# Two heads at a time in the attention and state space parts, and the last layer norm in a written order of VectorE

## The chip, the cores and the metric

One core of one Trainium2 chip runs the whole program in one launch. The metric is the device time in microseconds (us). The kernel before took 1444.42 us, the median of three runs (1443.53 to 1445.5).

## The reference

256 tokens of width 1024 pass through two blocks, all in f32.

The first block has two layers. Each takes a modulation vector from a condition (`w_ada`), normalizes, and runs a mixer whose one input projection feeds three parts; their outputs are concatenated, multiplied by `w_out`, and followed by an MLP with a squared relu.

```python
# differential attention: 4 heads, two softmaxes each over 32-wide q and k, values 64 wide
p = softmax(mask(q1 @ k1.T * scale)) - lam * softmax(mask(q2 @ k2.T * scale));  y_a = rmsnorm(p @ v)
# latent attention (MLA): 4 heads, scores of a 64-wide and a 32-wide rotary part
sc = (qn @ kn.T + qr @ kr.T) * scale;                  y_b = softmax(mask(sc)) @ v
# state space: 8 heads of 64, two groups, after a convolution, with a decay per head
y_c = ((cc @ bc.T) * exp(decay of the head)) @ (xs * dt) + ...
y = concatenate([y_a, y_b, y_c]) @ w_out
```

The mask lets a query see keys of its own and earlier chunks of 64. The second block runs three branches (an RWKV7 scan; attention of 8 heads of 64 with a distance penalty, called `moba`; a diagonal state space model), merges them with gates, and adds a layer norm, 32 experts in 4 groups with two chosen per token, and a last layer norm over the 1024 columns:

```python
y = (x - mean) * rsqrt(var + 1e-5) * w + b
```

## The kernel before

Tokens stand as columns (256 of them, `T`) and features as the 128 partitions (`P`) in most tensors; scores and the last layer norm have tokens on the partitions. Weights come from HBM on SP's queue in units of 1 MB (`raw`); ScalarE rounds each to a high part (`whi`) and VectorE subtracts to get the low part (`wlo`), and a product is three matmuls of these parts (`xh,whi`, `xh,wlo`, `xl,whi`). A *strip* is 128 output features, 24 such matmuls. Products without such parts are plain f32 matmuls, and each of those leaves two records on TensorE in the trace, one per pass; a bf16 matmul (the masks) leaves one.

The instructions of each engine are put in order by a planner, by what their operands wait for and by the place where they were traced. An instruction that is *pinned* (`pin`, L371) stays behind the instruction traced before it on its engine; `inorder(1)` pins TensorE's matmuls and transposes, `inorder()` pins all. All pass through helpers, whose lines are the ones that the profile shows: `act` L379 (ScalarE), `tt` L382, `ts` L386/387, `stt` L390 (VectorE), `mm` L393, `tr` L401 (TensorE).

A causal score matrix of 256 x 256 is kept as a tile of 128 x 384: 128 columns for the first half of the queries, 256 for the second. One head's scores are two f32 matmuls (`scores`, L925), 128 and 256 columns; the masks are two bf16 matmuls of one row (`chunkmask`, L919). `soft` (L910) takes two maxima on VectorE and two exponentials with accumulated sums on ScalarE. `pv` (L930) transposes the probabilities in three blocks, copies them out of PSUM by ScalarE (`at_pT`), and multiplies by the head's 64 value columns in two matmuls, into one half of the rows of an output tile `o`.

In the mixer (`_mixer`), the order of tracing is: input strips, the MLA projections, the state space matrix, the convolution with its transposes (`xd`), then MLA (L1130 to 1152), where after each two heads a strip of differential q and one of k are traced; a modulation vector (`adas`), the values v (`va`), the differential attention (L1175 to 1196), four strips of z, another modulation vector, and the state space heads (L1225 to 1246) with an exponent product `cs`, two masks, three exponentials, one multiplication (`ssE`) and two products each; then `w_out`. PSUM has eight buffers there, two each of the tags d (strips), s (scores), t (transposes) and o (outputs). `moba` (L1644) does the same for its heads, with a strip of q and of k before each two heads; after the scores there are two bf16 matmuls for the penalty (`mb_ak`) and two for the mask (`c4b`).

The tail of `moe` (L2612 to 2633) has the last layer norm, four quarters of 128 x 512 in PSUM (two halves of the tokens, `i`, by two halves of the columns, `h`). Statistics come first; for three quarters ScalarE subtracts the mean and GpSimd multiplies by w; then the reciprocal root (`rsqrt`, L556, a row of small VectorE steps in three rounds), and four fused operations add b, each with a write to HBM behind it, in the order (1,1), (0,0), (1,0), (0,1).

Of the kernel before, what the change touches and what calls it, by code (L numbers as in the profile page):

```python
# [26 lines left out]
BF = mybir.dt.bfloat16  # L27
I32 = mybir.dt.int32
AF = mybir.ActivationFunctionType
OP = mybir.AluOpType  # L30
# [4 lines left out]
P = 128  # L35
T = 256
# [275 lines left out]
class Prog:  # L312
# [603 lines left out]
        self.act(e[:, 0:P], sc[:, 0:P], AF.Exp, bias=mx[:, 0:1], scale=scale, accum=sm[:, j:j + 1])  # L916
        self.act(e[:, P:384], sc[:, P:384], AF.Exp, bias=mx[:, 1:2], scale=scale, accum=sm[:, j + 1:j + 2])

    def chunkmask(self, sc, r):  # L919

        for o in (0, 256):
            self.mm(sc[:, o:o + P], self.B("cm_q")[r:r + 1], self.B("cm_k")[r:r + 1], start=False, stop=True,
                    skip_group_check=True)

    def scores(self, sc, q, k, first, last=False):  # L925

        self.mm(sc[:, 0:P], q[:, 0:P], k[:, 0:P], start=first, stop=last, skip_group_check=True)
        self.mm(sc[:, P:384], q[:, P:T], k[:, 0:T], start=False, stop=last, skip_group_check=True)

    def pv(self, pool, p, v, vcol, o, half):  # L930

        tp = self.pt([P, 384], "t")
        for b in range(3):
            self.tr(tp[:, b * P:(b + 1) * P], p[:, b * P:(b + 1) * P])
        pT = self.sb(pool, [P, 384], "at_pT", bufs=2)

        self.act(pT, tp)
        oo = o[64 * half:64 * half + 64]
        self.mm(oo[:, 0:T], v[:, 0, vcol:vcol + 64], pT[:, 0:T], start=True, stop=False)
        self.mm(oo[:, P:T], v[:, 1, vcol:vcol + 64], pT[:, T:384], start=False, stop=True)  # L940


    def mixconst(self, l):
# [28 lines left out]
    def _mixer(self, pool, l, xT, pre, fill, n):  # L972
# [154 lines left out]
        sc96 = 96.0 ** -0.5  # L1127
        o = None

        def mla_head(h, o):  # L1130
            s, a = divmod(h, 2)
            sc = self.pt([P, 384], "s")
            r0 = slice(64 * a, 64 * a + 64)
            r1 = slice(32 * h, 32 * h + 32)
            self.scores(sc, qn[r0, s], kn[r0, s], True)
            self.scores(sc, qr[r1], krr[r1], False)
            self.chunkmask(sc, 32 * h)
# [6 lines left out]
            self.pv(pool, e, vb, 64 * h, o, a)  # L1144
# [29 lines left out]
        nsq = sb([P, 4, T], "nsq")  # L1174
        for s in range(2):  # L1175
            o = self.pt([P, T], "o")
            for a in range(2):
                sm = sb([P, 4], "at_s", bufs=3)
                es = []
                for m in range(2):  # L1180
                    sc = self.pt([P, 384], "s")
                    r = slice(64 * a + 32 * m, 64 * a + 32 * m + 32)
                    self.scores(sc, qa[r, s], ka[r, s], True)
                    self.chunkmask(sc, 64 * a + 32 * m)
                    e = sb([P, 384], "at_e", bufs=3)
                    self.soft(pool, sc, sc32, e, sm, 2 * m)
# [6 lines left out]
                self.pv(pool, es[0], va, 64 * (2 * s + a), o, a)  # L1193
# [30 lines left out]
        nsq = sb([P, 4, T], "nsq")  # L1224
        for s in range(4):  # L1225
            po = self.pt([P, T], "o")
            for a in range(2):
                h = 2 * s + a
                pe = self.pt([P, 384], "s")
                neg, idb = self.B("causnegT"), self.B("ident")  # L1230
                self.mm(pe, self.i8[0:40, h:h + 1].to_broadcast([40, P]), cs, start=True, stop=False,
                        skip_group_check=True)
                self.mm(pe[:, 0:P], idb, neg, start=False, stop=True, skip_group_check=True)
                self.mm(pe[:, T:384], idb, neg, start=False, stop=True, skip_group_check=True)
                E = sb([P, 384], "ssE", bufs=2)
                self.act(E[:, 0:P], pe[:, 0:P], AF.Exp, bias=nA[:, h:h + 1])
                self.act(E[:, P:T], pe[:, P:T], AF.Exp, bias=nA[:, 16 + h:17 + h])
                self.act(E[:, T:384], pe[:, T:384], AF.Exp, bias=nA[:, 8 + h:9 + h])
                self.tt(E, E, G[:, h // 4], OP.mult)
                oo = po[64 * a:64 * a + 64]  # L1240
                self.mm(oo, xd[:, 0, h], E[:, 0:T], start=True, stop=False, skip_group_check=True)
                self.mm(oo[:, P:T], xd[:, 1, h], E[:, T:384], start=False, stop=True,
                        skip_group_check=True)
            self.stt(yc[:, s], xbc[:, 2 + s], self.col(f"dskip{l}", s), po, OP.mult, OP.add)
            self.stt(yc[:, s], yc[:, s], 0.5, zs[:, s], OP.mult, OP.mult)
            self.act(nsq[:, s], yc[:, s], AF.Square)
# [397 lines left out]
    def moba(self, pool, X, y):  # L1644
# [6 lines left out]
        for s in range(4):  # L1651
# [4 lines left out]
            ps = self.strip(("in2", 2304 + P * s), X)  # L1656
            nc.vector.tensor_copy(k, ps)
            o = self.pt([P, T], "o")
            for a in range(2):
                h = 2 * s + a  # L1660
                r = slice(64 * a, 64 * a + 64)
                sc = self.pt([P, 384], "s")
                self.scores(sc, q[r], k[r], True)
                aq, ak = self.B("al_q"), sb([2, T], "mb_ak", BF, 2)
                self.ts(ak, self.B("al_k")[0:2], 2.0 ** -(h + 1), None, OP.mult)
                self.mm(sc[:, 0:P], aq[0:2, 0:P], ak[0:2, 0:P], start=False, stop=False, skip_group_check=True)
                self.mm(sc[:, P:384], aq[0:2, P:T], ak[0:2, 0:T], start=False, stop=False,
                        skip_group_check=True)
                for c in (0, 256):
                    self.mm(sc[:, c:c + P], self.B("ident"), self.B("causneg"), start=False, stop=True,  # L1670
                            skip_group_check=True)
                e = sb([P, 384], "at_e", bufs=3)
                sm = sb([P, 4], "at_s", bufs=3)
                self.soft(pool, sc, 0.125, e, sm, 0)
# [3 lines left out]
                self.pv(pool, e, v, 64 * h, o, a)  # L1678
            self.hl(y[0][:, s], y[1][:, s], o)

    def rwkv_start(self, pool, tmp, X):
# [917 lines left out]
    def moe(self, keep, thp, x2, xh, xl, route, dp, out):  # L2599
# [3 lines left out]
        with self.psum("pe", q=4, d=1, y=2, a=1):  # L2603
# [8 lines left out]
            st = self.sb(keep, [P, 2, 2, 6], "ln_st")  # L2612
            mv = self.sb(keep, [P, 2, 2], "ln_mv")
            neg = self.sb(keep, [P, 2], "ln_neg")
            zt = [self.sb(thp, [P, 1024], k) for k in ("gh", "gl")]
            half = lambda t, h: t[:, 512 * h:512 * h + 512]
            for i, h in ((0, 0), (1, 0), (0, 1), (1, 1)):
                nc.vector.bn_stats(st[:, i, h], z[i][h])  # L2618
                if h:
                    nc.vector.bn_aggr(mv[:, i], st[:, i])  # L2620
                    self.ts(neg[:, i:i + 1], mv[:, i, 0:1], -1.0, None, OP.mult)
            for i, h in ((0, 0), (1, 0), (0, 1)):
                o = half(zt[i], h)
                self.act(o, z[i][h], AF.Identity, bias=neg[:, i:i + 1])
                nc.gpsimd.tensor_tensor(o, o, half(w, h), op=OP.mult)
            self.ordered = 2
            y = self.rsqrt(keep, mv[:, :, 1], 2, 1.0, 1e-5)
            for i, h in ((1, 1), (0, 0), (1, 0), (0, 1)):
                o = half(zt[i], h)
                if i and h:  # L2630
                    self.stt(o, z[i][h], mv[:, i, 0:1], half(w, h), OP.subtract, OP.mult)
                self.stt(o, o, y[:, i:i + 1], half(b, h), OP.mult, OP.add)
                (nc.scalar if h else nc.sync).dma_start(half(out[i * P:(i + 1) * P], h), o)

# [29 lines left out]
```

## Time and profile before

| | |
|---|---|
| device time, median of three (range) | 1444.42 us (1443.53 to 1445.5) |
| profiled execution: device time, span | 1441.92 us, 1440.1 us |
| instructions | 26492 |
| mean granted TensorE clock | 0.98 of full speed |
| HBM read, mean rate over the span | 306.46 MB, 215 GB/s |

The page gives busy times and shares of the span for each engine: PE is TensorE's matmuls, PEld its weight loads, DVE VectorE, ACT ScalarE, POOL GpSimd. The layers' mixers stand at about 60 to 200 and 430 to 560 us, the second block's attention at 866 to 916, the experts from about 1100 to 1425, the last layer norm behind them. A row of a timeline is a run of alike instructions: start and length in us, engine, line, operation, output<-inputs, shapes and count; runs overlap, because matmuls are pipelined.

### The profile page before, as it was taken

The numbers are of one execution on the slowest core, as the hardware profiler recorded it, in microseconds if no ns is written. First come the engines' busy times: TensorE is split into PE (matmuls) and PEld (weight loads), VectorE is DVE, ScalarE is ACT, GpSimd is POOL, SyncE is SP. The second block draws the span as 40 slices with busy tenths as digits, with TensorE's granted clock in tenths as the row PEclk, the third lists the DMA queues.
The fourth block names the chain that finished last, engine by engine and source line by source line (L and its number), as shares of the span: only waits on it lengthen the run. The fifth ranks groups of instructions, "written<-read, shape, count | busy, mean of one in ns | idle before, by whom it ended". The sixth has DMA issues, their size and how long they took to land. (4 is left out here: it accounts for less than half of the span.)

```text
span 1440.1 us, 26492 instructions
## 1 busy us (share of the span) xinstructions
PE 1360.6 (94%) x10795; PEld 1117.6 (78%) x10795; DVE 864.5 (60%) x2012; ACT 651.9 (45%) x1307; POOL 48.5 (3%) x87
## 2 busy tenths in 40 slices
PE   3899999999999999999999989999998989999995
PEld 1787789999988877999997978888987864454442
DVE  2676677555578667999856555567646662232224
ACT  1665456444556645665555445354242441221121
POOL 0000000000000000000201010000000012000001
PEclk8999999999999999999999999999999999999998
DMA  9745467665565247455773234242124969999980
GB/s 370 291 158 205 180 245 300 231 247 192 188 243 217 98 166 280 166 186 180 167 246 125 89 133 147 88 147 90 56 92 174 404 203 401 419 409 373 395 323 31
DMA packets 45998, 311.70 MB, mean 216 GB/s; under 512 B 5296, under 2 KB 5744, under 8 KB 9648
## 3 DMA queue, kind: packets, MB, share of 16 engines
q1 hardware_dynamic: 41264, 293.10, 53.7%
q0 software_dynamic: 3312, 13.50, 3.5%
q10 hardware_dynamic: 1296, 3.36, 0.6%
q8 instruction: 87, 1.43, 0.4%
q14 instruction: 39, 0.32, 0.1%
HBM read 306.46 MB, written 3.47 MB: 215 GB/s over the span
## 5 line engine op out<-in xcount | busy, mean ns | idle before, releaser
L382 DVE TENSOR_TENSOR wlo<-raw,whi 128x1024 fp32r<-128x1024 f32 (+3 forms) x292 | 329.2, 1130 | 184.2 <-ACT whi L379 179.1
L379 ACT ACTIVATE whi<-raw 128x1024 fp32r<-128x1024 f32 (+3 forms) x292 | 284.4, 978 | 267.4 <-PE ps_d L393 191.8
L393 PE MATMUL ps_d<-xh,whi 128*128 128x256 f32 (+1 forms) x1072 | 308.6, 289 | 1.6 <-ACT whi L379 0.9
L393 PE MATMUL ps_d<-xh,wlo 128*128 128x256 f32 x816 | 234.3, 287 | 3.3 <-DVE wlo L382 3.2
L393 PE MATMUL ps_d<-xl,whi 128*128 128x256 f32 x816 | 232.9, 286 | 0.0
L393 PEld LDWEIGHTS ps_d<-xh,whi 128*128 128x128 f32 x1072 | 205.0, 191 | 7.4 <-issue 2.5
L393 PEld LDWEIGHTS ps_d<-xh,wlo 128*128 128x128 f32 x816 | 155.8, 191 | 6.5 <-DVE wlo L382 4.9
L393 PEld LDWEIGHTS ps_d<-xl,whi 128*128 128x128 f32 x816 | 155.8, 191 | 1.5 <-issue 1.2
L393 PE MATMUL ps_q<-ml_l,whi 128*128 128x256 f32 x512 | 143.7, 282 | 0.7 <-DVE ml_l L382 0.7
L393 PE MATMUL ps_q<-ml_h,wlo 128*128 128x256 f32 x512 | 143.1, 282 | 0.5 <-DVE wlo L382 0.5
L393 PE MATMUL ps_q<-ml_h,whi 128*128 128x256 f32 x512 | 143.1, 282 | 0.4 <-DVE ml_v L382 0.2
L393 PE MATMUL ps_d<-raw,xg 128*64 128x512 f32 x488 | 110.0, 595 | 1.0 <-DVE xg L387 1.0
L393 PEld LDWEIGHTS ps_q<-ml_h,whi 128*128 128x128 f32 x512 | 96.0, 188 | 1.8 <-ACT whi L379 0.6
L393 PEld LDWEIGHTS ps_q<-ml_l,whi 128*128 128x128 f32 x512 | 96.4, 188 | 1.1 <-DVE ml_l L382 1.1
L393 PEld LDWEIGHTS ps_q<-ml_h,wlo 128*128 128x128 f32 x512 | 96.1, 188 | 0.7 <-DVE wlo L382 0.7
L390 DVE SCALAR_TENSOR_TENSOR ex_t<-ex_t,ps_d 128x256 f32<-128x256 f32 x16 | 6.7, 421 | 134.7 <-ACT ex_t L379 134.7
L393 PEld LDWEIGHTS ps_d<-raw,xg 128*64 128x64 f32 x488 | 34.1, 137 | 68.6 <-issue 65.8
L393 PE MATMUL ps_d<-u,whi 128*128 128x258 f32 x256 | 73.8, 293 | 0.0
L393 PE MATMUL ps_d<-u,wlo 128*128 128x258 f32 x256 | 68.7, 287 | 0.3 <-DVE wlo L382 0.3
L393 PE MATMUL ps_d<-raw,cnd_s 128*32 128x256 f32 x768 | 52.4, 406 | 13.6 <-DVE cnd_s L386 11.1
L379 ACT ACTIVATE ex_t<-ps_d 128x256 f32<-128x256 f32 x16 | 6.1, 384 | 128.7 <-PE ps_d L393 128.7
L393 PE MATMUL ps_y<-raw,ex_hT 128*64 128x512 f32 x256 | 57.7, 592 | 0.0
(779 smaller groups left out, 2606.9 us busy)
## 6 DMA issues: line engine op xcount, KB each, us to landing
raw<-W SPq DMA_DIRECT2D x277, 1024.0 KB, 7.1
s5TP<-s5kd POOLq DMA_DIRECT2D x8, 256.0 KB, 15.5
th<-rows POOLq DMA_DIRECT2D x2, 1024.0 KB, 8.6
raw<-W SPq DMA_DIRECT2D x4, 512.0 KB, 10.1
xT<-xT ACTq DMA_DIRECT2D x1, 1024.0 KB, 20.0
xd<-xT POOLq DMA_DIRECT2D x1, 1024.0 KB, 4.8
th<-W POOLq DMA_DIRECT2D x1, 1024.0 KB, 5.1
xg<-W POOLq DMA_DIRECT2D x1, 1024.0 KB, 6.3
```

Of the source, the lines that this page charges most:

```text
L379: return self.pin(self.nc.scalar.activation(out, in_, f, bias=bias, scale=scale))
L382: return self.pin(self.nc.vector.tensor_tensor(out, a, b, op=op))
L390: return self.pin(self.nc.vector.scalar_tensor_tensor(out, a, s, b, op0=op0, op1=op1))
L393: i = self.nc.tensor.matmul(out, l, r, start=start, stop=stop, **k)
```

## The change

`scores`, `chunkmask` and `pv` take two heads. Scores of two heads stand in two PSUM tiles that are in use at once, the matmuls of the two alternate, the second head's first, and these matmuls are pinned. `pv` is a generator: it takes the two heads' probabilities one after the other and transposes each, then copies both in two pieces (`at_pT`, `at_pU`), and alternates the products on the two halves of the value columns; these are not pinned. MLA computes the second pair's scores ahead of the first pair's products. The differential attention writes all four score tiles of two heads before the first softmax. The state space heads go two by two, with one multiplication for both. The last layer norm is pinned throughout: one quarter goes by ScalarE and GpSimd, three by VectorE ahead of the root, and the writes go out in order of the rows.

```diff
-    def chunkmask(self, sc, r):
...
+    def chunkmask(self, sc, rows):
+        with self.inorder(1):
+            for o in (0, 256):
+                for s, r in list(zip(sc, rows))[::-1]:
+                    self.mm(s[:, o:o + P], self.B("cm_q")[r:r + 1], self.B("cm_k")[r:r + 1], start=False, stop=True,
+                            skip_group_check=True)
+    def scores(self, sc, q, k, first):
+        two = list(zip(sc, q, k))[::-1]
+        with self.inorder(1):
+            for s, a, b in two:
+                self.mm(s[:, 0:P], a[:, 0:P], b[:, 0:P], start=first, stop=False, skip_group_check=True)
+            for s, a, b in two:
+                self.mm(s[:, P:384], a[:, P:T], b[:, 0:T], start=False, stop=False, skip_group_check=True)
+    def pv(self, pool, v, vcol, o, tag="t"):
+        pa, pb = self.pt([P, 2, T], tag), self.pt([P, 2, P], tag)
+        for a in range(2):
+            p = yield
+            for b in range(2):
+                self.tr(pa[:, a, b * P:(b + 1) * P], p[:, b * P:(b + 1) * P])
+            self.tr(pb[:, a], p[:, T:384])
+        ta, tb = self.sb(pool, [P, 2, T], "at_pT"), self.sb(pool, [P, 2, P], "at_pU")
+        self.act(ta, pa)
+        self.act(tb, pb)
+        oo = [o[64 * a:64 * a + 64] for a in range(2)]
+        c = [slice(vcol + 64 * a, vcol + 64 * a + 64) for a in range(2)]
+        for a in range(2):
+            self.mm(oo[a][:, 0:T], v[:, 0, c[a]], ta[:, a], start=True, stop=False, skip_group_check=True)
+        for a in range(2):
+            self.mm(oo[a][:, P:T], v[:, 1, c[a]], tb[:, a], start=False, stop=True, skip_group_check=True)
+        yield
...
+        def mla_scores(s):
+            sc = [self.pt([P, 384], "st"[s]) for _ in range(2)]
...
+        sc = mla_scores(0)
         for s in range(2):
+            e = [mla_soft(sc.pop(0)) for _ in range(2)]
+            if s == 0:
+                sc = mla_scores(1)
             o = self.pt([P, T], "o")
-            for a in range(2):
-                mla_head(2 * s + a, o)
+            f = self.pv(pool, vb, 128 * s, o, "st"[s])
+            next(f)
+            while e:
+                f.send(e.pop(0))
...
         for s in range(2):
             o = self.pt([P, T], "o")
+            g = "st"[s], "ts"[s]
+            sc = []
+            for a in range(2):
+                r = [64 * a, 64 * a + 32]
+                sc.append([self.pt([P, 384], g[a]) for _ in range(2)])
+                self.scores(sc[a], [qa[i:i + 32, s] for i in r], [ka[i:i + 32, s] for i in r], True)
+                self.chunkmask(sc[a], r)
...
+                if a == 0:
+                    f = self.pv(pool, va, 128 * s, o, g[0])
+                    next(f)
+                f.send(es[0])
...
+            E = sb([P, 2, 384], "ssE", bufs=2)
+            pe = [self.pt([P, 384], "s") for _ in range(2)]
+            for a in (1, 0):
+                h = 2 * s + a
+                self.mm(pe[a], self.i8[0:40, h:h + 1].to_broadcast([40, P]), cs, start=True, stop=False,
+                        skip_group_check=True)
...
+            self.tt(E, E, G[:, s // 2:s // 2 + 1].to_broadcast([P, 2, 384]), OP.mult)
+            for a in range(2):
+                self.mm(po[64 * a:64 * a + 64], xd[:, 0, 2 * s + a], E[:, a, 0:T], start=True, stop=False,
                         skip_group_check=True)
+            for a in range(2):
+                self.mm(po[64 * a:64 * a + 64, P:T], xd[:, 1, 2 * s + a], E[:, a, T:384], start=False, stop=True,
                         skip_group_check=True)
...
+            sc = [self.pt([P, 384], "s") for _ in range(2)]
+            r = [slice(64 * a, 64 * a + 64) for a in range(2)]
+            self.scores(sc, [q[i] for i in r], [k[i] for i in r], True)
+            aq = self.B("al_q")
+            self.ordered = 1
...
-            for i, h in ((0, 0), (1, 0), (0, 1)):
-                o = half(zt[i], h)
-                self.act(o, z[i][h], AF.Identity, bias=neg[:, i:i + 1])
-                nc.gpsimd.tensor_tensor(o, o, half(w, h), op=OP.mult)
-            self.ordered = 2
+        with self.inorder():
+            for h in range(2):
+                for i in range(2):
+                    self.pin(nc.vector.bn_stats(st[:, i, h], z[i][h]))
+            for i in (1, 0):
+                self.pin(nc.vector.bn_aggr(mv[:, i], st[:, i]))
+                if i:
+                    neg = self.sb(keep, [P, 1], "ln_neg")
+                    self.ts(neg, mv[:, 1, 0:1], -1.0, None, OP.mult)
+            o = half(zt[1], 1)
+            self.act(o, z[1][1], AF.Identity, bias=neg)
+            self.pin(nc.gpsimd.tensor_tensor(o, o, half(w, 1), op=OP.mult))
+            for i, h in ((0, 0), (0, 1), (1, 0)):
+                self.stt(half(zt[i], h), z[i][h], mv[:, i, 0:1], half(w, h), OP.subtract, OP.mult)
             y = self.rsqrt(keep, mv[:, :, 1], 2, 1.0, 1e-5)
-            for i, h in ((1, 1), (0, 0), (1, 0), (0, 1)):
...
+            for i in range(2):
+                for h in range(2):
+                    o = half(zt[i], h)
+                    self.stt(o, o, y[:, i:i + 1], half(b, h), OP.mult, OP.add)
+                    (nc.scalar if h else nc.sync).dma_start(half(out[i * P:(i + 1) * P], h), o)
```

## Rows read from the trace of the kernel before

**Rows 1.** The page's part 1: busy us of each engine (share of the span), instructions.
```profile
PE 1360.6 (94%) x10795; PEld 1117.6 (78%) x10795; DVE 864.5 (60%) x2012; ACT 651.9 (45%) x1307; POOL 48.5 (3%) x87
```
**Rows 2.** Stretches: us, busy PE PEld DVE ACT POOL, PE clock, DMA share, GB/s.
```profile
82.00:200.00 118.00, 117.67 (x937) 94.19 (x937) 77.10 (x211) 64.78 (x166) 0.50 (x5) 1.00 0.50 189
...
450.00:560.00 110.00, 107.68 (x831) 87.62 (x829) 74.38 (x188) 61.98 (x161) 4.92 (x5) 1.00 0.43 147
...
866.00:916.00 50.00, 49.44 (x367) 41.07 (x366) 25.61 (x72) 23.12 (x59) 0.00 (x0) 1.00 0.27 99
...
1100.00:1425.00 325.00, 314.50 (x1676) 178.02 (x1676) 122.14 (x307) 82.69 (x149) 16.92 (x21) 0.99 0.85 338
```
**Rows 3.** TensorE's timeline (start, length, operation, shapes): an MLA head; last xd transposes.
```profile
86.97 0.92 PE L393 MATMUL ps_s<-kn,qn 64*128 64x128 f32 x4
87.82 0.92 PE L393 MATMUL ps_s<-krr,qr 32*128 32x128 f32 x4
88.58 0.27 PE L393 MATMUL ps_s<-c0b 1*128 1x128 bf16 x2
88.78 0.92 PE L393 MATMUL ps_s<-kn,qn 64*128 64x128 f32 x4
...
94.33 0.38 PE L401 MATMUL ps_t<-c,xbc 128*128 128x128 f32 x2
```
**Rows 4.** TensorE's timeline: the products of the first two MLA heads.
```profile
99.91 0.91 PE L393 MATMUL ps_o<-at_pT,vb 128*64 128x256 f32 x8
```
**Rows 5.** TensorE's timeline: two differential scores one after the other.
```profile
132.13 1.03 PE L393 MATMUL ps_s<-ka,qa 32*128 32x128 f32 x7
132.89 0.27 PE L393 MATMUL ps_s<-c0b 1*128 1x128 bf16 x2
133.01 0.37 PE L393 MATMUL ps_s<-ka,qa 32*128 32x256 f32 x1
133.31 0.55 PE L401 MATMUL ps_t<-c,at_e 128*128 128x128 f32 x3
```
**Rows 6.** TensorE's timeline: the state space matrix, from both halves of the rows.
```profile
70.76 0.92 PE L393 MATMUL ps_s<-xbc 64*128 64x128 f32 x6
```
**Rows 7.** TensorE's timeline: a state space head's exponent and products, then the next exponent.
```profile
154.42 0.43 PE L393 MATMUL ps_s<-cs,i 40*128 40x384 f32 x1
...
155.00 0.86 PE L393 MATMUL ps_o<-ssE,xd 128*64 128x256 f32 x4
155.80 0.44 PE L393 MATMUL ps_s<-cs,i 40*128 40x384 f32 x1
```
**Rows 8.** TensorE's timeline: scores of two heads of the second attention.
```profile
893.93 0.92 PE L393 MATMUL ps_s<-mb_k,mb_q 64*128 64x128 f32 x4
...
895.26 0.92 PE L393 MATMUL ps_s<-mb_k,mb_q 64*128 64x128 f32 x4
```
**Rows 9.** The tile at_e: ns shortest/median/longest, the stretch, shapes.
```profile
L378 ACT ACTIVATE at_e<-ps_s,at_mx x64: 350/420/490, 92.0 to 909.0; 128x128 f32<-128x128 f32 x32, 128x256 f32<-128x256 f32 x32
L378 ACT ACTIVATION_READ_ACCUMULATOR at_e<-ps_s,at_mx x64: 190/200/224, 92.2 to 909.3; 128x1 f32 x64
```
**Rows 10.** VectorE's timeline at the end: the reciprocal root and the products after it.
```profile
1428.27 0.16 DVE L387 TENSOR_SCALAR rs_v<-ln_mv 128x2 f32<-128x2 f32 x1
...
1429.13 2.48 DVE L390 SCALAR_TENSOR_TENSOR rs_t<-rs_y,rs_v 128x1 f32<-128x1 f32 x2
...
1433.20 0.74 DVE L390 SCALAR_TENSOR_TENSOR gl<-ps_q,ln_mv,th 128x512 f32<-128x512 f32 x1
...
1435.98 0.75 DVE L390 SCALAR_TENSOR_TENSOR gh<-gh,rs_y,th 128x512 f32<-128x512 f32 x1
```
**Rows 11.** GpSimd's timeline: products at 1193 and at the end.
```profile
1193.52 10.42 POOL L2435 TENSOR_TENSOR th<-th,th 128x512 f32<-128x512 f32 x8 [8.43 <-DMA th<-rows]
...
1429.12 1.25 POOL L2625 TENSOR_TENSOR gh<-gh,th 128x512 f32<-128x512 f32 x1 [224.28 <-ACT gh L379]
```
**Rows 12.** VectorE's timeline: an operation with a PSUM operand beside those GpSimd products.
```profile
1197.93 0.75 DVE L390 SCALAR_TENSOR_TENSOR gl<-ps_y,ws,gh 128x512 fp32r<-128x512 f32 x1 [1.12 <-ACT gh L379]
```

More of the change, by code (lines that the diff above doesn't have):

```diff
@@ L917, in soft @@
         self.act(e[:, P:384], sc[:, P:384], AF.Exp, bias=mx[:, 1:2], scale=scale, accum=sm[:, j + 1:j + 2])
-    def chunkmask(self, sc, r):
[L921 to L940, printed above, removed]
+    def chunkmask(self, sc, rows):
[4 more added lines that the diff above has]
+                            skip_group_check=True)
@@ L1128, in _mixer, with mla_soft @@
         o = None
[L1130 to L1137, printed above, removed]
+        def mla_scores(s):
+            sc = [self.pt([P, 384], "st"[s]) for _ in range(2)]
+            r0 = [slice(64 * a, 64 * a + 64) for a in range(2)]
+            r1 = [slice(64 * s + 32 * a, 64 * s + 32 * a + 32) for a in range(2)]
+            self.scores(sc, [qn[r, s] for r in r0], [kn[r, s] for r in r0], True)
+            self.scores(sc, [qr[r] for r in r1], [krr[r] for r in r1], False)
+            self.chunkmask(sc, [64 * s, 64 * s + 32])
+            return sc
+        def mla_soft(sc):
             e = sb([P, 384], "at_e", bufs=3)
@@ L1143, in mla_head @@
             self.ts(e[:, P:384], e[:, P:384], sm[:, 1:2], None, OP.mult)
-            self.pv(pool, e, vb, 64 * h, o, a)
+            return e
+        sc = mla_scores(0)
         for s in range(2):
+            e = [mla_soft(sc.pop(0)) for _ in range(2)]
+            if s == 0:
+                sc = mla_scores(1)
             o = self.pt([P, T], "o")
-            for a in range(2):
-                mla_head(2 * s + a, o)
+            f = self.pv(pool, vb, 128 * s, o, "st"[s])
+            next(f)
+            while e:
+                f.send(e.pop(0))
+            f = None
             self.hl(yh[:, 2 + s], yl[:, 2 + s], o)
@@ L1180, in _mixer @@
                 for m in range(2):
[L1181 to L1184, printed above, removed]
                     e = sb([P, 384], "at_e", bufs=3)
-                    self.soft(pool, sc, sc32, e, sm, 2 * m)
+                    self.soft(pool, sc[a].pop(0), sc32, e, sm, 2 * m)
                     es.append(e)
@@ L1230, in _mixer @@
-                neg, idb = self.B("causnegT"), self.B("ident")
-                self.mm(pe, self.i8[0:40, h:h + 1].to_broadcast([40, P]), cs, start=True, stop=False,
-                        skip_group_check=True)
[L1233 to L1242, printed above, removed]
+                self.mm(pe[a][:, 0:P], idb, neg, start=False, stop=True, skip_group_check=True)
@@ new lines, in _mixer @@
+                self.mm(pe[a][:, T:384], idb, neg, start=False, stop=True, skip_group_check=True)
+            for a in range(2):
+                h = 2 * s + a
+                for c, b in ((slice(0, P), 0), (slice(P, T), 16), (slice(T, 384), 8)):
+                    self.act(E[:, a, c], pe[a][:, c], AF.Exp, bias=nA[:, b + h:b + h + 1])
+            self.tt(E, E, G[:, s // 2:s // 2 + 1].to_broadcast([P, 2, 384]), OP.mult)
+            for a in range(2):
+                self.mm(po[64 * a:64 * a + 64], xd[:, 0, 2 * s + a], E[:, a, 0:T], start=True, stop=False,
+                        skip_group_check=True)
@@ L1243, in _mixer @@
+            for a in range(2):
+                self.mm(po[64 * a:64 * a + 64, P:T], xd[:, 1, 2 * s + a], E[:, a, T:384], start=False, stop=True,
                         skip_group_check=True)
+            pe = None
             self.stt(yc[:, s], xbc[:, 2 + s], self.col(f"dskip{l}", s), po, OP.mult, OP.add)
@@ L1658, in moba @@
             o = self.pt([P, T], "o")
-            for a in range(2):
[L1660 to L1667, printed above, removed]
+            sc = [self.pt([P, 384], "s") for _ in range(2)]
[3 more added lines that the diff above has]
+            self.ordered = 1
+            for a in range(2):
+                ak = sb([2, T], "mb_ak", BF, 2)
+                self.ts(ak, self.B("al_k")[0:2], 2.0 ** -(2 * s + a + 1), None, OP.mult)
+                self.mm(sc[a][:, 0:P], aq[0:2, 0:P], ak[0:2, 0:P], start=False, stop=False, skip_group_check=True)
+                self.mm(sc[a][:, P:384], aq[0:2, P:T], ak[0:2, 0:T], start=False, stop=False,
                         skip_group_check=True)
+            for a in range(2):
                 for c in (0, 256):
-                    self.mm(sc[:, c:c + P], self.B("ident"), self.B("causneg"), start=False, stop=True,
+                    self.mm(sc[a][:, c:c + P], self.B("ident"), self.B("causneg"), start=False, stop=True,
                             skip_group_check=True)
+            self.ordered = 0
+            f = self.pv(pool, v, 128 * s, o)
+            next(f)
+            for a in range(2):
                 e = sb([P, 384], "at_e", bufs=3)
                 sm = sb([P, 4], "at_s", bufs=3)
-                self.soft(pool, sc, 0.125, e, sm, 0)
+                self.soft(pool, sc[a], 0.125, e, sm, 0)
                 nc.vector.reciprocal(sm[:, 0:2], sm[:, 0:2])
@@ L1677, in moba @@
                 self.ts(e[:, P:384], e[:, P:384], sm[:, 1:2], None, OP.mult)
-                self.pv(pool, e, v, 64 * h, o, a)
+                f.send(e)
+            f = e = sc = None
             self.hl(y[0][:, s], y[1][:, s], o)
@@ L2611, in moe @@
                 self.overflow(q, rd, x2, cnt, z)
[L2612 to L2621, printed above, removed]
@@ L2622, in moe @@
-            for i, h in ((0, 0), (1, 0), (0, 1)):
-                o = half(zt[i], h)
-                self.act(o, z[i][h], AF.Identity, bias=neg[:, i:i + 1])
-                nc.gpsimd.tensor_tensor(o, o, half(w, h), op=OP.mult)
-            self.ordered = 2
-            y = self.rsqrt(keep, mv[:, :, 1], 2, 1.0, 1e-5)
-            for i, h in ((1, 1), (0, 0), (1, 0), (0, 1)):
[L2629 to L2633, printed above, removed]
+            self.lastnorm(keep, thp, z, w, b, out)
@@ new lines, in lastnorm @@
+    def lastnorm(self, keep, thp, z, w, b, out):
+        nc = self.nc
+        st = self.sb(keep, [P, 2, 2, 6], "ln_st")
+        mv = self.sb(keep, [P, 2, 2], "ln_mv")
+        zt = [self.sb(thp, [P, 1024], k) for k in ("gh", "gl")]
+        half = lambda t, h: t[:, 512 * h:512 * h + 512]
+        with self.inorder():
[12 more added lines that the diff above has]
+                self.stt(half(zt[i], h), z[i][h], mv[:, i, 0:1], half(w, h), OP.subtract, OP.mult)
+            y = self.rsqrt(keep, mv[:, :, 1], 2, 1.0, 1e-5)
+            for i in range(2):
[3 more added lines that the diff above has]
+                    (nc.scalar if h else nc.sync).dma_start(half(out[i * P:(i + 1) * P], h), o)
```

4 lines of the change are left out of this document (2 added, 2 removed).

## The prediction

> **What bounds the kernel now.** I read the page's engine line first. TensorE is busy 94% of the span, VectorE 60%, ScalarE 45% [rows 1], so the first question is where TensorE is the limit. The view by stretches answers it: in both mixers TensorE is busy 117.67 of 118 us and 107.68 of 110, in the second block's attention 49.44 of 50, while VectorE and ScalarE stand near two thirds there and the DMA at half or less [rows 2]. In these stretches a microsecond of TensorE is a microsecond of the kernel. In the experts' stretch the DMA's share is 0.85 [rows 2]; that work begins when the stage before it has ended, so time saved earlier moves it forward and does not change its length. The last stretch, some 15 us, belongs to VectorE. Then I read TensorE's timeline, in which the price of an item is the time from its row's start to the start of the next row. An f32 matmul leaves two records, one for each pass of its weights, so "x4" is one head's two matmuls.
>
> **Prices before.** One latent-attention (MLA) head costs 0.85 us for its 64-row scores, 0.76 for its 32-row scores and 0.20 for its masks, 1.8 together [rows 3]. A state space head costs 0.58 for the decay's exponent with its masks, and 0.80 for its two products of 64 columns [rows 7]. A head of the second block's attention costs 1.33 for everything ahead of the softmax [rows 8].
>
> **What pairing is worth.** Products on two halves of the columns: the planner already laid the first MLA pair of a layer in the order that the change writes. Its eight records take 0.91 us, where four records of a single pair member take 0.86 [rows 4, 7]; the second head is nearly free, and a pair falls from 1.60 to 0.85, by 0.75. Scores on two groups of rows: six records of the state space matrix, from two halves of the rows, take 0.92, as long as the four records of one head [rows 3, 6]; and two 32-row heads that the planner put one after the other took 1.18 with one head's masks among them, 1.07 without [rows 5]. Bounds for a pair are thus 0.85 (second head free) and 1.70 (no overlap). I take 0.95, nearest to rows 5 and 6, for 64 rows and 0.86 for 32.
>
> The rows also show that TensorE keeps no strict order there: the two masks start between the seventh and the eighth record of the 32-row scores, hence between two passes of one matmul [rows 5]. The Trainium skill, "TensorE: Matmul & The Clock Gate", Part 3 (The mechanism), states the contrary, that matmuls start and end strictly in order. By that rule alternating heads overlap only by single passes, which is a rival below.
>
> **The sum, per mixer layer.**
> MLA scores and masks: a pair falls from 2 x 1.81 = 3.6 to 0.95 + 0.86 + about 0.3 for four masks = 2.1; two pairs, 3.0 us. MLA products: one of the two pairs is not yet paired, 0.75.
> Differential attention scores: eight softmaxes at 0.96 (0.76 and 0.20, the prices of rows 3) make 7.7, less about 0.8 for those already overlapped as in rows 5 (two pairs in one layer, one in the other): 6.9. After: four pairs at 0.86 + 0.3 = 4.7. Saved 2.2. Products: two pairs, 1.5.
> State space: four pairs of products, 3.0. The exponent's two matmuls of a pair have the same rows, so they do not overlap; standing side by side they save a change of shape and back, which I take as 0.3 of 0.58 (bounds 0 and 0.58): 1.1.
> Together 11.6 a layer, 23.2 for two. Second block's attention: four pairs, scores from 2.66 to 1.63 (0.95, and twice 0.48, which is 1.33 less 0.85, less the changes of shape), 4.1; products, three pairs' worth as one and a half already overlap, 1.7: 5.8. **TensorE sum: 29.0 us.**
>
> What it adds. ScalarE copies the transposes once a pair in two pieces instead of once a head: no fewer columns, off the bound. One multiplication over both heads of E replaces two on VectorE; nothing waits for the difference, because TensorE has the output projection to do. The written order, however, ties a pair's first score matmul behind the matmul traced before it. For the first MLA pair this is the last transpose of the convolved channels, which ran at 94.33, while the scores began at 86.97 [rows 3]. TensorE has the next strip of weights (24 matmuls) to do meanwhile, but VectorE must finish the convolution before it splits the strip after that; I take 1.2 us idle a layer, bounds 0 (strips cover it) and 7.4 (none does). The first differential pair is tied behind the transposes of v, the second behind the products of the first; z's four strips and a modulation vector cover these, and I take 1.0 a layer. Minus 4.4.
>
> The last layer norm. From the first instruction of the reciprocal root to the first product after it VectorE takes 4.93 us [rows 10]. Its first step and round take 0.86 (1428.27 to 1429.13), so three rounds at half of that each, with the 0.4 ahead of them, would be 1.8; the rest is three small instructions that stood until GpSimd's product was over, as at 1429.13 [rows 10, 11]. The change leaves one GpSimd product and puts three fused operations (0.7 each, from the last rows: 2.78 over four) ahead of the root. They read z from PSUM, and such an operation took its usual 0.75 at 1197.93 inside GpSimd's 10 us of products [rows 11, 12], so I cost the collision at nothing (bounds 0 and 1.25). The last write then starts after 0.2 + 2.1 + 1.8 + 2.1 = 6.2 us, where it took 7.7 (1428.27 to 1435.98): minus 1.5.
>
> **Sum:** 29.0 - 4.4 + 1.5 = 26.1 us. The profiled execution took 1441.92 us around its span of 1440.1, so 1415.8; the median of the three runs is 1444.42, 2.5 above, and I give 1418.
>
> **Rivals.**
> Strict order. By the rule above, a pair of scores costs about 1.17 (an estimate: eight passes, one of each head overlapping) instead of 0.95: 20 pairs lose 4.4 us, 1422. For it speaks that rows 5 show only neighbouring heads, not alternating ones; against it the masks' place. 0.10.
> The differential part becomes bound by its chain. Four score tiles now take every buffer of both PSUM tags, and the second group of heads must wait for the first one's products. Each exponential takes 0.42 and its accumulator's read 0.20, two of each a softmax [rows 9]: 5.0 us of ScalarE a group, and as much again for maxima, combination, transposes and copies, so some 12 a group and 24 a layer. If the strips just cover it, the differential gain (3.7 a layer) is lost: 1425.5. The Trainium skill's "TensorEngine Tiling (Array Packing)", PSUM Bottleneck, warns of this in general, that packing leaves the evacuation of PSUM as it was. 0.17.
> The other side: slower. The same 24 us of a layer stand open, because the planner has spent z's strips on earlier bubbles; then TensorE has only its own 7 us in them and idles 17. Two layers cost 34 against 26.1: 1452. It decides from 13 us of idle a layer on. Against it: the planner fills a bubble only where there would be idleness anyway, and TensorE stands still less than 2.4 us in either mixer now [rows 2]. 0.08.
> The pairs are torn apart again: nothing in the products is tied, so other matmuls may come between, and each head pays as before; only the norm's gain stays, 1442.9. Against it the planner's own pair in rows 4. 0.05.
>
> **How the numbers follow.** The forecast has 0.60, with 1409 to 1427 for itself: scores at 0.85 and no idleness give 8 us more, pairs at 1.07 with twice the idleness 9 less. A range of 1407 to 1434 takes in the first two rivals and leaves out most of the last two. 0.2% (2.9 us) is what this kernel's measurement tells from no change: faster 0.86 (forecast and two rivals), same 0.06, slower 0.08.
>
> **What would show it.** In the changed trace: score groups of eight records as long as those of four; 64-column products always in eights; both mixers about 10 us shorter with TensorE still near 99% busy; the second attention 5 to 6 shorter; one GpSimd product in the tail and no small VectorE operation above 0.3 us. Wrong if TensorE's stretches hold idle time of more than 5 us a layer, ended by exponentials or by copies of transposes, or if single heads' records stand apart.

## The result and the profile after

The changed kernel took 1424.86 us (median; 1413.19 to 1429.87), the kernel before beside it 1443.97: a ratio of 0.9849, 95% interval 0.9811 to 0.9886. Another set of rounds gave 1423.54 and 0.9852 (0.9807 to 0.9896). The prediction was 1418 (1407 to 1434): the median lies inside the range and 7 us above the centre. The profiled execution took 1413.19 around a span of 1411.3, so the profile shows 28.8 us less and the median some 20; most of this section and the next is about that difference.

The page's engines, and the same four stretches as in [rows 1, 2], moved to where their work now stands (the columns of rows 2: us, busy PE PEld DVE ACT POOL, granted clock, DMA share, GB/s):

```profile
PE 1325.2 (94%) x10795; PEld 1095.8 (78%) x10795; DVE 862.5 (61%) x2005; ACT 646.6 (46%) x1305; POOL 46.2 (3%) x85
```
```profile
80.00:189.00 109.00, 105.38 (x933) 87.00 (x931) 75.51 (x206) 63.00 (x166) 0.50 (x5) 0.97 0.54 201
440.00:545.00 105.00, 100.37 (x865) 83.94 (x863) 78.70 (x207) 61.54 (x163) 4.92 (x5) 1.00 0.49 178
847.00:893.00 46.00, 44.01 (x367) 37.95 (x366) 26.45 (x75) 23.00 (x61) 0.00 (x0) 1.00 0.31 108
1073.00:1398.00 325.00, 314.19 (x1676) 177.75 (x1675) 121.94 (x307) 82.81 (x149) 17.20 (x21) 0.99 0.86 338
```

TensorE has as many instructions and is busy 35 us less. The experts' stretch is as long as it was, 27 us earlier. The mixers now hold 3.6 and 4.6 us without a matmul (TensorE is busy 97% and 96%, not near 99% as forecast), and the first one is not at the full clock. TensorE's timeline answers to rows 3, 4 and 8 (MLA scores of two heads, their products, then the scores of the second attention):

```profile
92.68 0.93 PE L393 MATMUL ps_s<-kn,qn 64*128 64x128 f32 x8
93.54 0.92 PE L393 MATMUL ps_s<-krr,qr 32*128 32x128 f32 x8
94.30 0.28 PE L393 MATMUL ps_s<-c0b 1*128 1x128 bf16 x4
94.50 1.48 PE L393 MATMUL ps_t<-kn,qn 64*128 64x128 f32 x8
...
99.87 0.65 PE L393 MATMUL ps_o<-at_pT,vb 128*64 128x256 f32 x4
100.35 0.39 PE L393 MATMUL ps_o<-at_pU,vb 128*64 128x128 f32 x4
100.67 0.39 PE L393 MATMUL ps_d<-u,wlo 128*128 128x258 f32 x1
...
882.27 0.93 PE L393 MATMUL ps_s<-mb_k,mb_q 64*128 64x128 f32 x8
883.13 0.50 PE L393 MATMUL ps_s<-mb_ak,c4b 2*128 2x128 bf16 x4
```

Eight records take what four took: 0.86 for two 64-row heads (92.68 to 93.54), 0.76 for two 32-row heads, 0.80 for a pair's products. The second head is free. The second MLA pair is the exception (1.41, 94.50 to 95.91): its second head's first record starts at 95.06, because VectorE reads the transposes out of the buffer that this head needs until 95.01:

```profile
93.73 1.28 DVE L382 TENSOR_TENSOR xd<-ps_t,dt 128x512 f32<-128x512 f32 x2
```

In the differential part the gain is larger than one free head:

```profile
119.51 0.71 PE L393 MATMUL ps_s<-ka,qa 32*128 32x128 f32 x6
119.85 0.58 PE L393 MATMUL ps_t<-ka,qa 32*128 32x128 f32 x2
120.06 0.38 PE L393 MATMUL ps_s<-ka,qa 32*128 32x256 f32 x2
120.06 0.49 PE L393 MATMUL ps_t<-ka,qa 32*128 32x128 f32 x3
120.27 0.28 PE L393 MATMUL ps_s<-c0b 1*128 1x128 bf16 x4
120.38 0.59 PE L393 MATMUL ps_t<-ka,qa 32*128 32x256 f32 x3
120.61 0.48 PE L393 MATMUL ps_t<-c0b 1*128 1x128 bf16 x4
121.02 0.39 PE L393 MATMUL ps_d<-xh,whi 128*128 128x258 f32 x1
```

Four softmaxes with all their masks take 1.51 us (119.51 to 121.02); four times the price of rows 3 (0.96) is 3.8. The second group's scores (`ps_t`) start at 119.85, ahead of the first group's masks (120.27), which the kernel writes first and which are pinned.

The waits of TensorE in the first mixer (what it waited for, us in total, times, longest) are new; in the kernel before there was one, of 0.3:

```profile
PE ps_t L401 <- ACT un_c L379: 1.6, 1, 1.6
PE ps_s L401 <- DVE at_e L386: 0.9, 1, 0.9
PE ps_s L401 <- DVE at_e L390: 0.7, 1, 0.7
PE ps_d L393 <- DVE pn_t L382: 0.4, 1, 0.4
```

The end, VectorE's and then GpSimd's timeline, answers to rows 10 and 11:

```profile
1401.51 1.41 DVE L390 SCALAR_TENSOR_TENSOR gh<-ps_q,ln_mv,th 128x512 f32<-128x512 f32 x2
1402.84 0.74 DVE L390 SCALAR_TENSOR_TENSOR gl<-ps_q,ln_mv,th 128x512 f32<-128x512 f32 x1
1403.50 0.16 DVE L387 TENSOR_SCALAR rs_v<-ln_mv 128x2 f32<-128x2 f32 x1
...
1405.26 1.41 DVE L390 SCALAR_TENSOR_TENSOR gh<-gh,rs_y,th 128x512 f32<-128x512 f32 x2
```
```profile
1402.22 1.26 POOL L2676 TENSOR_TENSOR gl<-gl,th 128x512 f32<-128x512 f32 x1 [224.44 <-ACT gl L379]
```

The root takes 1.76 us (1403.50 to 1405.26) where it took 4.93, and the operation at 1402.84 is not stretched by the product beside it.

**By stage**, us between the same two matmuls of each trace; the last column is from the start of the last matmul to the end:

| | first mixer | second mixer | second attention | end |
|---|---|---|---|---|
| before | 113.48 | 110.03 | 59.81 | 14.87 |
| changed, first profile | 105.17 | 100.15 | 54.65 | 13.14 |
| changed, profile of the second rounds | 103.06 | 101.53 | 60.80 | 13.13 |
| forecast, saved | 9.4 | 9.4 | 5.8 | 1.5 |

The two profiles of the changed kernel are of the same instructions. Taking each stage where its clock was full, 10.4, 9.9, 5.2 and 1.7 were saved: 27.2 against a forecast of 26.1. (Of the first profile's 28.8 us, 2.1 stand ahead of the first changed instruction, so they are not the change's.) Of the stages that differ, the second attention is the plainest. First profile, then the other, over its end:

```profile
884.00:889.00 5.00, 3.35 (x25) 2.38 (x26) 2.70 (x12) 2.59 (x10) 0.00 (x0) 1.00 0.00 0
889.00:894.00 5.00, 5.00 (x47) 4.83 (x44) 2.11 (x5) 1.53 (x3) 0.00 (x0) 1.00 0.02 3
```
```profile
885.00:890.00 5.00, 3.35 (x23) 2.38 (x23) 2.81 (x12) 2.59 (x10) 0.00 (x0) 0.97 0.00 0
890.00:895.00 5.00, 5.00 (x27) 4.45 (x23) 0.42 (x1) 0.38 (x1) 0.00 (x0) 0.50 0.02 3
```

Both have the same two waits there (0.9 for the last softmax, 0.64 for the copy of its transposes; 3.35 of 5 us busy), and in one of them the clock falls to its lower level behind them (0.50 for 13.65 us), and 27 matmuls take the time of 47. The stage costs 6.15 us more. In the first mixer of the first profile the clock fell likewise, inside the state space heads:

```profile
141.00:147.40 6.40, 6.40 (x47) 4.02 (x44) 3.62 (x12) 4.48 (x15) 0.00 (x0) 1.00 0.96 370
147.40:154.20 6.80, 6.75 (x32) 4.20 (x31) 4.52 (x15) 4.03 (x14) 0.00 (x0) 0.50 0.41 167
```

Ahead of this fall TensorE had waited 1.6 us, then done 32-column matmuls, transposes and 64-column products; no strip of weights stood among them from 141 to 152.

### The profile page after: what moved, and what is told of

It reads as the page before. It is cut to its first block, busy times and chain, and to the rows that moved or that the text cites. A ratio compares the mean times of both kernels' runs of the same rounds, so it can differ in the third digit from the quotient of the medians.

```text
span 1411.3 us, 26443 instructions
## 1 busy us (share of the span) xinstructions
PE 1325.2 (94%) x10795; PEld 1095.8 (78%) x10795; DVE 862.5 (61%) x2005; ACT 646.6 (46%) x1305; POOL 46.2 (3%) x85
## 6 DMA issues: line engine op xcount, KB each, us to landing
raw<-W SPq DMA_DIRECT2D x4, 512.0 KB, 10.4
```

## The experiments

Each is an edit of the changed kernel unless it says otherwise. "At like clock" is from one line fitted through all 116 runs (7.4 us for 0.01 of mean clock, one offset for each kernel), against the kernel before, with twice the standard error. That all kernels share one slope is an assumption.

**The changed kernel once more.**

> The changed kernel once more, in more rounds, to see how its times spread. The trace's span fell by 28.8 us, the median of the first runs only by 19 to 22. If the spread is one of the granted clock that meets every kernel alike, the ratio to the kernel before comes out near 0.982 (26 us less), with the times of either kernel falling along its mean clock. If the denser pairs themselves cost clock, the changed kernel's runs stand at a lower mean clock than the runs of before, and the ratio stays at 0.985 or above.

Ratio 0.9852. Mean clock over its ten runs 0.9741, over 46 of the kernel before 0.9782 (difference 0.0041, twice its error 0.0036): on the edge of what can be told, and worth 3 us. At like clock it is 25.2 (±1.9) faster. So at like clock the forecast's 26.1 is within the error, and the clock, if its difference is real, takes 3 us of it back.

**The last layer norm alone**, on the kernel before (`self.lastnorm(...)` in place of the tail).

> The kernel before with the new last layer norm alone. My term: 1.5 us less. From the last matmul to the end of the span 14.9 us become 13.1 to 13.4, GpSimd has one product there, and no small VectorE operation of the root lasts above 0.3 us. Nothing else moves. Rival (the collision only moves to the three fused operations that read PSUM beside GpSimd's product): 14.9 stays within 0.4, and one of the three lasts above 1.1 us.

13.14 us behind the last matmul, 14.87 before; 1442.44, ratio 0.9973 (0.9944 to 1.0002). The term is right in the trace, and too small for the ratio; at like clock it shows as 2.0 (±1.7).

**Heads one after the other, still pinned.**

```diff
             for s, a, b in two:
                 self.mm(s[:, 0:P], a[:, 0:P], b[:, 0:P], start=first, stop=False, skip_group_check=True)
-            for s, a, b in two:
                 self.mm(s[:, P:384], a[:, P:T], b[:, 0:T], start=False, stop=False, skip_group_check=True)
```

> The changed kernel with the score and mask matmuls of a pair written head after head, still pinned, not alternating; everything else as changed. If TensorE works on groups of rows independently and takes the next head's passes as soon as its rows are free, eight records of a pair still take about 0.85 to 1.05 us and the time stays within 3 us of the changed kernel. If TensorE starts matmuls strictly in order, only the passes at the seam between two heads overlap: a 64-row pair takes about 1.5 us, a 32-row pair 1.3, and the kernel loses about 5 us a layer and 2.6 in the second attention, some 12 us over the changed kernel.

1424.25, ratio 0.9842 (0.9801 to 0.9884), and the timeline's rows are those of the alternating order:

```profile
93.71 0.93 PE L393 MATMUL ps_s<-kn,qn 64*128 64x128 f32 x8
94.57 0.93 PE L393 MATMUL ps_s<-krr,qr 32*128 32x128 f32 x8
```

Taken one by one, the first record of the head that is written second starts 13 ns behind the first record of the other, 0.3 us ahead of that one's second matmul, which the program has before it. The rival of the strict order falls. The Trainium skill, "TensorE: Matmul & The Clock Gate", Part 3 (The mechanism), says that matmuls start in program order; on disjoint rows they do not here.

**Products one head after the other.**

> The changed kernel with the products of a pair written head after head (all 64-column products of attention and state space), not alternating. If TensorE takes the other half of the columns as soon as it is free, as it took the other rows, a pair of attention products stays at 0.80 us and the state space products at 3.2 to 3.6 us a layer. If the order counts here, the two passes pairs of one head share a half of the columns and do not overlap: a pair costs up to 1.6 again, the state space products 6.4 a layer, together up to 5.5 us a layer and 3.2 in the second attention.

```profile
100.13 0.71 PE L393 MATMUL ps_o<-at_pT,vb 128*64 128x256 f32 x3
100.61 0.27 PE L393 MATMUL ps_o<-at_pU,vb 128*64 128x128 f32 x1
100.67 0.38 PE L393 MATMUL ps_o<-at_pT,vb 128*64 128x256 f32 x1
100.72 0.55 PE L393 MATMUL ps_o<-at_pU,vb 128*64 128x128 f32 x3
101.20 0.38 PE L393 MATMUL ps_d<-u,wlo 128*128 128x258 f32 x1
```
```profile
99.97 0.38 ACT L379 ACTIVATE at_pU<-ps_s 128x256 f32<-128x256 f32 x1
```

This kernel has one run (1430.65 us at a clock of 0.970), so no ratio. The pair takes 1.07, between 0.80 and 1.60, and what holds the second head is a wait. The first head's second matmul reads `at_pU`, whose copy ScalarE ends at 100.35; the second head, written behind that matmul, starts at 100.41. In eleven of the twelve attention pairs the second head starts 0.06 us behind the end of this copy. In the twelfth the copy was ready before the pair began (499.53 and 499.64), and there, as in seven of the eight state space pairs, the second head starts 13 ns behind the first and overlaps it in full. So two halves of the columns overlap as two groups of rows do, but a matmul that waits for its operand holds up the ones written behind it. Alternating puts that wait where it costs nothing: a quarter of a microsecond a pair here.

**No pins on scores and masks** (`inorder(0)`).

> The changed kernel with the pins taken off the score and mask matmuls; the traced order and the buffers stay. My term for the ties was 4.4 us of idle TensorE, so 2 to 4 us less than the changed kernel if the planner keeps the pairs together and fills the bubbles. Rival: without the pins the planner puts other matmuls between the heads, pairs are torn apart, and up to 10 us come back. Third possibility: nothing (within 2 us), when the bubbles come from the chain of exponentials and not from the ties.

1421.14, ratio 0.9820 (0.9777 to 0.9863). Idle time falls from 3.6 and 4.6 us to 2.4 and 1.8, but the four softmaxes of a group come apart, one run of scores at 120.65 and the next at 124.62 with strips between them, and the differential scores cost 4.51 us a layer, not 1.96:

```profile
120.65 1.03 PE L393 MATMUL ps_t<-ka,qa 32*128 32x128 f32 x6
121.41 0.27 PE L393 MATMUL ps_t<-c0b 1*128 1x128 bf16 x2
...
124.62 0.48 PE L393 MATMUL ps_t<-ka,qa 32*128 32x128 f32 x2
```

At like clock both kernels are alike (24.6 ±2.5 against 25.2 ±1.9): the ties cost about what they bring. The stages at full clock agree: both mixers together 204.35 us, with ties 203.21.

**The first matmul of a group unpinned.**

> The changed kernel with the pin taken off the first score matmul of a group only (each pair in MLA and the second attention, each group of four softmaxes in the differential part); the rest of the group stays pinned behind it. My theory now: the ties to what was traced before cost the idle time (3.5 and 4.2 us in the two mixers of the changed trace, 0.7 without pins), the pins inside a group give the overlap of four heads (1.96 us a layer for all differential scores, 4.51 without pins). Then idle falls to about 1 us a layer, the scores stay at about 2.0, and the kernel gains 4 to 6 us over the changed one. Rival: the group waits for its last buffer anyway, and the idle time moves inside the group: no gain within 2 us.

The 0.7 us of idle time that this text gives for the kernel without pins is wrong (2.4 and 1.8, above), so there was less to win than it says. There was no gain, as the rival had it: idle time fell to 1.9 and 2.2 us, but other work went between the first matmul and the rest, and the differential scores cost 3.55 a layer. It took 1426.61, ratio 0.9886 (0.9831 to 0.9940), at the lowest mean clock of all that were repeated (0.969); at like clock it is 24.9 (±3.0) faster than the kernel before, like the changed kernel.

**The exponent's two matmuls on different rows.**

> The changed kernel with the decay's cumulated sums held twice, in rows 0 to 39 and 64 to 103, so that the exponent's two matmuls of a pair read different rows; two more small matmuls a layer make the second copy. If sharing rows is what kept these matmuls apart (2.75 to 3.44 us a layer for eight), a pair takes about 0.4 and a layer 1.5 to 1.8, less 0.3 for the copy: 2 us less over both layers. If the whole 128 columns that each writes are what keeps them apart, nothing is gained and 0.6 us is lost.

1424.80, ratio 0.9844 (0.9788 to 0.9901): no gain. Where the two matmuls of a pair stood side by side, they did overlap; the same pair in the changed kernel, and here:

```profile
497.18 0.61 PE L393 MATMUL ps_s<-cs,i 40*128 40x384 f32 x2
497.73 0.40 PE L393 MATMUL ps_s<-c0b 128*128 128x128 bf16 x4
```
```profile
499.01 0.44 PE L393 MATMUL ps_s<-cs,i 40*128 40x384 f32 x2
499.39 0.40 PE L393 MATMUL ps_s<-c0b 128*128 128x128 bf16 x4
```

0.55 becomes 0.38. This is one pair: these matmuls are not pinned, the other seven pairs stood apart, and a pair that stands apart gains nothing.

**Other buffers for the last transposes of the second attention** (`self.pv(pool, v, 128 * s, o, "ts"[s == 3])`, both softmaxes ahead of it).

> The changed kernel with the last pair of the second attention using the scores' PSUM buffers for its transposes, so that the router's transposes that come next need not wait for theirs. In the changed trace TensorE stood 0.9 us for the last softmax and 0.64 for its copy there. Expected: both waits gone, 1.5 us less, and the second attention at the full clock in its profile; in two profiles of three the clock fell to half for 13.65 us right behind these waits. Rival: the router's transposes are not ready either, and the waits stay.

The wait of 0.9 is 0.3, that of 0.64 stays, and two new waits, 0.9 together, stand behind them for the parts of the next strips, so the stage is as long (54.66); 1420.57, ratio 0.9826 (0.9778 to 0.9875).

**Which part lets the clock fall.** Among the eight profiles of all kernels here that have both tied differential groups and state space pairs, twelve of sixteen mixers had a fall inside the state space heads (one of four in the changed kernel's own two profiles). So these two were undone, one at a time.

> The changed kernel with the state space heads one by one again, as in the kernel before; all else as changed. In five of eight profiles of kernels with the pairs the clock fell to half behind the differential part, at about 148 us in the first mixer, and in five of eight at about 500 in the second (3.4 to 13.7 us each time); in neither profile of a kernel without pairs. First theory: the thin stretch ahead of it does that (strips spent, 32-column matmuls, transposes, 1.6 us idle). Then these falls stay, the mean clock stays near 0.974, and the time is 6 us above the changed kernel (3.1 a layer for the products), near 1430. Rival: the paired state space products do it. Then the falls there go, the mean clock rises to 0.977 or more, and the time is the changed kernel's or below.

> The changed kernel with the differential scores one softmax after the other again, in the two score buffers, as in the kernel before; its products stay paired, all else as changed. First theory: TensorE's scores cost 3.6 us a layer more, but the strips last longer, idle time falls from 3.6 to 4.6 us a mixer to 1 to 2, the falls of the clock behind the differential part go, and the mean clock rises to 0.977 or more: 1420 to 1424, no slower than the changed kernel. Rival (the state space pairs do it): the falls stay, the clock stays near 0.974, and the time is 2 to 5 us above the changed kernel.

Neither theory alone: in both kernels there was no fall in either mixer's state space heads, in one profile each. Single state space heads: 1426.17, ratio 0.9858 (0.9821 to 0.9895), 21.1 (±2.3) faster than before at like clock. Single differential softmaxes: 1425.63, the same ratio and interval, 21.6 (±2.3). Each undone part gives back about 4 us at like clock (±2.8), and the ratio is still the changed kernel's; the mean clock (0.977 in both, against 0.974) would account for 2 us, but that difference is within its noise (±0.005). Nor is the thin stretch itself enough: with single heads the same idle 1.6 us stood ahead of it.

**Two kernels from these.**

> The unpinned kernel with the other buffers for the last pair's transposes in the second attention, as the best of what was tried: 1420 at a mean clock of 0.980, as the unpinned one, if falls of the clock behind the second attention are chance; below 1419 if the shorter wait keeps the clock there in every execution. The second attention at full clock in its profile speaks for the latter (four of nine profiles with the longer wait had a fall of 13.65 us there, that of the other buffers had none).

> The changed kernel with the other buffers, and pins only in the differential part: its scores keep the overlap of four heads (1.96 us a layer against 4.51 unpinned), and the latent attention's first wait (0.87 us a layer) should go. Undisturbed mixers of 102 and 99 us, against 103.1 and 100.2 with all pins and 105.2 and 99.2 without. If thin work ahead of the paired state space products lets the clock fall, the falls at about 148 and 500 us stay in this kernel, since the differential part's bubbles stay, and are rare in the unpinned one: then its mean clock stands at 0.977 or less, and its time is no better than the unpinned one's.

(By the traces the "four of nine" is six of nine.) No pins and the other buffers: 1414.81, ratio 0.9787 (0.9758 to 0.9815), mean clock 0.982, no fall in either mixer or in the second attention. It has the lowest time of all, but its interval overlaps those of the two kernels that it is made of, and its profile's stages are as long as without pins (105.27, 99.23 and 54.66 us against 105.19, 99.16 and 54.65). Against the changed kernel its clock is higher beyond the noise (by 0.008 ±0.0045, some 6 us), its work at like clock is not shown to be less (2.4 ±2.9). Pins in the differential part alone: 1419.87, ratio 0.9801 (0.9771 to 0.9830), with falls at 148 and 503 us and one of 10 us at 889, and a mean clock of 0.9755. At like clock the second is not told from the first (29.7 ±2.3 against 27.6 ±2.3), and it is 4.5 (±2.7) ahead of the changed kernel; its lower clock (by 0.007 ±0.004) costs it some 5 us against the first. The other buffers don't rule the fall in the second attention out: one of three profiles with them had it.

## Why the prediction held, term by term

The first mixer at full clock (for the changed kernel, its second profile), us of TensorE from start to next start with the waits taken out:

| step | before | changed | saved | forecast |
|---|---|---|---|---|
| MLA scores | 6.91 | 3.71 | 3.2 | 3.0 with their masks |
| MLA products | 2.43 | 1.60 | 0.8 | 0.75 |
| differential scores | 5.32 | 1.96 | 3.4 | 2.2 with their masks |
| differential products | 3.18 | 1.60 | 1.6 | 1.5 |
| state space products | 6.36 | 3.28 | 3.1 | 3.0 |
| state space exponent | 2.94 | 2.94 | 0.0 | 1.1 |
| all masks | 3.61 | 3.20 | 0.4 | |
| idle | 0.31 | 4.06 | -3.7 | -2.2 |

This adds to 8.8 of the stage's 10.4; the rest lies in the matmuls between and was not taken apart.

- Pairs: rows 4 to 6 were the right rows, and the lower bound (0.85, second head free) was the truth, but for the second MLA pair's 1.41. The differential scores were mis-sized because I counted pairs: four 32-row heads overlap.
- The exponent: nothing came of "standing side by side". A pair of them side by side took 0.55 where two apart take 0.74 (2.94 over eight), and mostly they stood apart.
- Idle: it grew by 3.7 and 2.4 us a mixer, more than 2.2 a layer, and not where I had put it. The first MLA pair, tied behind the last transposes of the convolution, follows them without a wait (92.68), so that term of 1.2 was nothing. Most of the waits stand ahead of the transposes of the probabilities, behind softmaxes and copies as the rival of the chain had it, but far from 13. Without pins 2.4 and 1.8 us of idle time remain, so the ties make about half of the increase in the first mixer and all of it in the second. The errors in size cancel (more gain from the scores than forecast, none from the exponent, more idle time): that the sum came so near is in this part luck.
- The second attention: scores and masks 10.18 to 5.98 (4.2, forecast 4.1), products 5.05 to 3.20 (1.85, forecast 1.7), and 1.0 of new waits that I had not put in; the numbers are worked out from the trace as in the table.
- The last layer norm: 1.7, forecast 1.5, and the collision with GpSimd costs nothing, as costed.
- The rivals: no strict order (above); the added waits, those of the differential part's chain among them, took 2.4 to 3.7 us a mixer, not the whole gain; pairs of scores came apart only where the ties were taken off; nothing was slower than the kernel before. The forecast's own bounds (8 us more, 9 less) are about 6 and 8 when worked out from its terms; nothing rests on them.
- What no step had: the clock. I priced every gap at its own length. Behind the new gaps the clock fell in some executions and not in others; whether it is the gaps that lower it stays open. The first profile caught a clock of 0.981 where ten runs of the changed kernel have 0.974 on average, 5 us by the fitted line; with the 2.1 us ahead of the change, that is most of why the median gained less than the profile. Against the kernel before the clock is worth some 3 us, on the edge of the noise.

## What to carry to other kernels

Here small matmuls on different rows of the array, or on different halves of its columns, overlapped in either written order, if nothing stood between them and none of them had to wait for its operand; so put them side by side, the ones whose operands are ready first, and count by groups of rows (the scores of four 32-row heads cost 1.0, not 2 x 0.76). Tie only what must stay together, and look at what the tie keeps waiting. On an engine with a clock that falls, compare two profiles of the same program, stage by stage, before believing either: the stage at full clock gives the price of the edit, the runs' mean clock what is left of it.

## What was not expected of the hardware

The same instructions with the same waits ran at the full clock in one execution and for 13.65 us at half of it in another (54.65 and 60.80 us). Behind the tied differential groups with paired state space heads the clock fell in twelve of sixteen mixers; with either part undone or the ties removed, or in the two kernels without pairs, in none of twelve. The stretch of the best kernel had products of the output projection among its state space pairs, that of the changed kernel had none until 152 us, but neither had the kernel with single heads; what decides is therefore open.
